# Block 1's mixer outputs are transposed through the bank of the projections' transposes

## The chip, the cores and the metric

The kernel runs on one core of a Trainium2 chip. The metric is the device time of one launch in microseconds (us), here on that one core. TensorE is called PE in the rows, VectorE DVE, ScalarE ACT, GpSimd POOL and SyncE SP; PEld is TensorE's weight load.

## The reference

The reference is a small transformer with two kinds of blocks over 1024 tokens of width 1024. Only the first kind ("block 1", two layers) matters here. In each of its layers a normed input goes through one wide projection, its columns feed three mixers, and the mixers' outputs stand side by side and go through the output projection:

```python
ATTN_W = 512; RET_W = 256; GLA_W = 256          # D_MIX = 1024
o = attention: softmax over a window of 128 keys, 8 heads of 64   # rotary on q and k, gate g
o = retention: 4 heads of 64, chunks of 128, fixed decay          # head norm, gate
o = gated_linear_attention: 4 heads (dk 32, dv 64), learned decay # head norm, gate
y = concat([attn, ret, gla]) @ w_out                              # then a norm and the residual
```

Every product is made of fp32 operands that are split into a high and a low part (three matmuls for one), so each operand that meets a weight exists as a pair: `hi` is a rounded copy and `lo` is what the copy lost.

## The kernel before, in words

A layer's 1024 tokens are worked in two halves of four token tiles of 128. So block 1 has four halves, in the order (layer 0, first), (layer 0, second), (layer 1, first), (layer 1, second). The block takes about the first 1300 us of the launch; what follows it has its own code and does not call the changed function.

For each half the host code writes out, in this order: `p_attn` (three projections: K and V, then Q, then the gate G), the output product of the half before (`finish`), `p_ret` (retention's projections), `p_gla` (the projections of gated linear attention, GLA, and between two of them `norm_T`, which norms and transposes the next half's input). The mixers themselves are generators: `s_attn`, `s_ret` and `s_gla` of a half are appended to a list, and after each k step of any projection `tick` runs one step of the generator that stands first. So GLA of one half is worked while the K, Q and G projections of the next half run. Priorities (`HP`, `HE`, `HX`) and a scheduler turn this into one fixed order of instructions for each engine.

When a token tile of a mixer is finished, `into` (L534) transposes it on PE into PSUM and `split` (L201) evacuates it twice: ACT casts it into the high part (L202), DVE subtracts that from PSUM for the low part (L203). It runs for 16 attention tiles (4 transposes each), 16 retention tiles and 16 GLA tiles (2 transposes each), 48 in all. The pair is called M, and the output product reads it.

PSUM has eight banks, and the tiles that share a tag take turns in its banks in the order in which the host code allocates them:

```python
mk("ps", {"mm": 4, "mt": 1, "sm": 2, "o": 1}, space=PSUM)     # L176
```

`mm` holds the four accumulators of a projection, one for each token tile. `sm` (two banks) holds the scores of the three mixers (L721, L726, L746, L846, L997), their state updates (L867, L1018) and, before the change, the 48 transposes of `into`. `mt` (one bank) holds the transposes of rotated queries and keys (L524 with source pe), the decays of GLA and the transposes of `norm_T` (L398). `o` holds the mixers' outputs.

Two more places matter below. When the Q projection ends, each token tile's query is rotated by DVE (`rotary`, twice per token tile, for two groups of heads: L650, L653 and L654 read the accumulator, L655 and L656 write the result) and then transposed through `mt`; the accumulator is free for the G projection after the second L654. The rotary uses the SBUF tag `pe`, which has three buffers: the result, and two of the products. And in `s_gla` the first two GLA tiles reach `into` while the host code is still in the Q projection of the next half, so they are allocated ahead of the queries' transposes.

Of the kernel before, what the change touches and what calls it, by code (L numbers as in the profile page):

```python
# [162 lines left out]
class Net:  # L163
# [369 lines left out]

    def into(self, mT, k0, t, src, n):  # L534
        hi, lo, _ = mT
        ps = self.transposes(None, src, n)
        ts_ = slice(t * P, (t + 1) * P)
        self.split(hi(k0, k0 + n)[:, :, ts_], lo(k0, k0 + n)[:, :, ts_], ps)

# [1190 lines left out]
```

## Time and profile before

| what | value |
|---|---|
| median of 3 runs | 3937.48 us (3937.02 to 3942.3) |
| the profiled execution | 3937.08 us, its span 3935.3 us |
| mean granted clock of PE | 0.986 of full speed |
| PE / DVE / ACT / POOL busy | 95% / 62% / 43% / 17% of the span |

The span runs from the first to the last instruction; the profiled execution's own time is 1.8 us longer and lies within the range of the three runs. The shares are averages over the launch.

### The profile page before, as it was taken

The numbers are of one execution on the slowest core, as the hardware profiler recorded it, in microseconds if no ns is written. First come the engines' busy times: TensorE is split into PE (matmuls) and PEld (weight loads), VectorE is DVE, ScalarE is ACT, GpSimd is POOL, SyncE is SP. The second block draws the span as 40 slices with busy tenths as digits, with TensorE's granted clock in tenths as the row PEclk, the third lists the DMA queues.
The fourth block names the chain that finished last, engine by engine and source line by source line (L and its number), as shares of the span: only waits on it lengthen the run. The fifth ranks groups of instructions, "written<-read, shape, count | busy, mean of one in ns | idle before, by whom it ended". The sixth has DMA issues, their size and how long they took to land. (4 is left out here: it accounts for less than half of the span.)

```text
span 3935.3 us, 55613 instructions
## 1 busy us (share of the span) xinstructions
PE 3726.1 (95%) x19144; PEld 3045.4 (77%) x19144; DVE 2445.6 (62%) x5209; ACT 1685.8 (43%) x3652; POOL 649.3 (17%) x1026
## 2 busy tenths in 40 slices
PE   7999999999999898899999999999899999999998
PEld 6877777877877787677887788888777788887886
DVE  7686787687687657576545643335765654455444
ACT  4443444454454555464334422224554543344333
POOL 2021134243252212131001000000311100001000
PEclk9999999999999999999999999999999999999999
DMA  6144344343343313333333632222412123334332
GB/s 213 50 134 121 113 143 121 109 129 110 105 136 98 103 56 107 108 108 105 126 102 110 209 110 68 62 66 89 145 54 86 69 64 97 97 100 166 97 97 94
DMA packets 249453, 420.37 MB, mean 107 GB/s; under 512 B 32002, under 2 KB 101203, under 8 KB 249171
## 3 DMA queue, kind: packets, MB, share of 16 engines
q1 hardware_dynamic: 241426, 389.52, 32.0%
q0 software_dynamic: 7744, 27.30, 1.9%
q8 instruction: 151, 2.47, 0.3%
q14 instruction: 132, 1.07, 0.1%
HBM read 389.42 MB, written 27.30 MB: 106 GB/s over the span
## 5 line engine op out<-in xcount | busy, mean ns | idle before, releaser
L203 DVE TENSOR_TENSOR wl<-wr,wh 128x512 fp32r<-128x512 f32 (+2 forms) x948 | 644.2, 682 | 812.9 <-ACT wh L202 809.4
L202 ACT CAST wh<-wr 128x512 fp32r<-128x512 f32 (+2 forms) x948 | 553.7, 585 | 1208.8 <-PE mm L502 489.8
L502 PE MATMUL mm<-wh,M 128*128 128x512 f32 (+1 forms) x2944 | 945.9, 393 | 24.6 <-ACT M L202 14.8
L502 PE MATMUL mm<-wh,H 128*128 128x512 f32 (+2 forms) x2432 | 791.5, 396 | 12.3 <-DVE pe L654 3.6
L506 PE MATMUL mm<-H,wh 128*128 128x512 f32 x2240 | 727.4, 395 | 1.8 <-ACT wh L202 1.7
L502 PEld LDWEIGHTS mm<-wh,M 128*128 128x128 f32 x2944 | 550.0, 190 | 142.8 <-ACT M L202 23.1
L502 PE MATMUL mm<-wl,M 128*128 128x512 f32 (+1 forms) x1472 | 576.0, 391 | 0.4 <-DVE wl L203 0.4
L502 PEld LDWEIGHTS mm<-wh,H 128*128 128x128 f32 x2432 | 450.0, 192 | 100.5 <-issue 4.7
L506 PEld LDWEIGHTS mm<-H,wh 128*128 128x128 f32 x2240 | 418.8, 189 | 82.2 <-ACT wh L202 2.0
L502 PE MATMUL mm<-wl,H 128*128 128x512 f32 (+2 forms) x1216 | 471.1, 388 | 0.0
L506 PE MATMUL mm<-H,wl 128*128 128x512 f32 x1120 | 444.5, 397 | 0.0
L502 PEld LDWEIGHTS mm<-wl,M 128*128 128x128 f32 x1472 | 279.8, 190 | 49.2 <-DVE wl L203 1.2
L502 PEld LDWEIGHTS mm<-wl,H 128*128 128x128 f32 x1216 | 234.0, 192 | 35.1 <-issue 0.2
L506 PEld LDWEIGHTS mm<-H,wl 128*128 128x128 f32 x1120 | 212.2, 189 | 37.2
L1398 PEld LDWEIGHTS o<-kv,pT 128*128 128x128 f32 x1280 | 158.1, 192 | 25.0 <-ACT pT L1394 20.4
L317 POOL TENSOR_TENSOR ac<-ac,aw 128x256 f32<-128x256 f32 x168 | 142.9, 851 | 162.8 <-ACT aw L316 143.9
L1398 PE MATMUL o<-kv,pT 128*128 128x64 f32 x1280 | 167.5, 274 | 1.6 <-ACT pT L1394 0.9
L311 DVE SCALAR_TENSOR_TENSOR ac<-aw,c,ac 128x256 f32<-128x256 f32 x280 | 160.1, 572 | 5.9 <-DMA aw<-in_w_ada 3.1
L1483 DVE TENSOR_TENSOR Z<-Z,mm 128x512 f32<-128x512 f32 x224 | 140.2, 681 | 2.8 <-PE mm L502 2.5
L558 POOL TENSOR_TENSOR tm<-tm 128x1 f32<-128x1 f32 x34 | 6.6, 196 | 763.3 <-ACT pe L553 762.9
L1375 DVE CUSTOM_DVE_ANT_0 p<-sm,c,c 128x384 f32<-128x384 f32 (+1 forms) x144 | 82.2, 571 | 76.0 <-PE sm L1373 74.5
L1381 ACT ACTIVATE p<-p,ti 128x640 f32<-128x640 f32 (+2 forms) x144 | 110.8, 770 | 43.1 <-DVE ti L1380 39.7
(353 smaller groups left out, 5703.1 us busy)
## 6 DMA issues: line engine op xcount, KB each, us to landing
wr<-in_w_ff SPq DMA_DIRECT2D x512, 256.0 KB, 2.7
wr<-in_w_in SPq DMA_DIRECT2D x240, 256.0 KB, 2.7
wr<-in_w_out SPq DMA_DIRECT2D x144, 256.0 KB, 2.7
x<-xd SPq DMA_DIRECT2D x64, 512.0 KB, 4.9
aw<-in_w_ada SPq DMA_DIRECT2D x192, 128.0 KB, 2.1
x<-in_w_ada SPq DMA_DIRECT2D x96, 256.0 KB, 2.9
xd<-x POOLq DMA_DIRECT2D x44, 512.0 KB, 3.8
wr<-in_w_in SPq DMA_DIRECT2D x152, 128.0 KB, 2.1
```

Of the source, the lines that this page charges most:

```text
L202: self.nc.scalar.copy(hi, src)
L203: self.nc.vector.tensor_sub(lo, src, hi.bitcast(F32))
L311: nc.vector.scalar_tensor_tensor(acc[:, 0], wt, c[0], acc[:, 0], ALU.mult, ALU.add)
L317: nc.gpsimd.tensor_tensor(acc[:, 1], acc[:, 1], wt, ALU.add)
L502: nc.tensor.matmul(acc[j][:, :ncol], lhsT=x[:, j * P:(j + 1) * P], rhs=y[:, :ncol], start=first, stop=last)
L506: nc.tensor.matmul(acc[j][:m, :w], lhsT=y[:, j * P:j * P + m], rhs=x[:, :w], start=first, stop=last)
L558: nc.gpsimd.tensor_tensor(ss[j][:, 0:1], ss[j][:, 0:1], ss[j][:, 1:2], ALU.add)
L1375: nc.vector.tensor_tensor_reduce(sc[:, at:at + w], ps[:, :w], mask, 1.0, prev, ALU.add, ALU.max, accum_out=acc)
L1381: nc.scalar.activation(sc[:, :at], sc[:, :at], AF.Exp, bias=nm, accum_out=den[:, h:h + 1])
L1398: nc.tensor.matmul(O[:, h * 64:h * 64 + 64], lhsT=pT[:, i, :], rhs=Vs(j)[:, sl], start=i == 0, stop=i == nk - 1)
L1483: nc.vector.tensor_add(y, y, ps)
```

## The change

`into` allocates its PSUM tile from the tag `mt` where it allocated it from `sm`. Nothing else is edited; the number of instructions and their shapes stay the same.

```diff
     def into(self, mT, k0, t, src, n):
         hi, lo, _ = mT
-        ps = self.transposes(None, src, n)
+        ps = self.transposes(None, src, n, tag="mt")
         ts_ = slice(t * P, (t + 1) * P)
         self.split(hi(k0, k0 + n)[:, :, ts_], lo(k0, k0 + n)[:, :, ts_], ps)
```

What moves is the order. DVE at the handover from the Q to the G projection of the second half, before (mm_2941 is the Q accumulator of token tile 1, pe_3316 its rotated query, sc_3163 a GLA output):

```order
L650 TENSOR_TENSOR pe_3317<-mm_2941,c_158 128x256
L653 TENSOR_TENSOR pe_3318<-mm_2941,c_160 128x4x32
L654 TENSOR_TENSOR pe_3318<-mm_2941,c_160 128x4x32
L655 TENSOR_TENSOR pe_3316<-pe_3317,pe_3318 128x4x32
L656 TENSOR_TENSOR pe_3316<-pe_3317,pe_3318 128x4x32
L827 TENSOR_TENSOR sc_3163<-sc_3163,ti_3169 128x256
L650 TENSOR_TENSOR pe_3324<-mm_2941,c_158 128x256
L653 TENSOR_TENSOR pe_3325<-mm_2941,c_160 128x4x32
L654 TENSOR_TENSOR pe_3325<-mm_2941,c_160 128x4x32
```

The same place on DVE now: the first L654 of that tile, the first two of the rows behind it, and the last ones up to its second L654:

```order
L654 TENSOR_TENSOR pe_3318<-mm_2941,c_160 128x4x32
L1021 SCALAR_TENSOR_TENSOR gs_2546<-gs_2547,ti_2550,sm_3157 32x64 x4
L820 TENSOR_TENSOR sc_3163<-o_3151,pu_2504 128x256
...
L203 TENSOR_TENSOR M_1108<-mt_3267,M_1107 128x2x128
L311 SCALAR_TENSOR_TENSOR ac_3230<-aw_3243,c_70,ac_3230 128x256
L1000 COPY_PREDICATED st_2966<-c_629,sm_3290 128x512
L655 TENSOR_TENSOR pe_3316<-pe_3317,pe_3318 128x4x32
L656 TENSOR_TENSOR pe_3316<-pe_3317,pe_3318 128x4x32
L311 SCALAR_TENSOR_TENSOR ac_3230<-aw_3246,c_70,ac_3230 128x256
L650 TENSOR_TENSOR pe_3324<-mm_2941,c_158 128x256
L653 TENSOR_TENSOR pe_3325<-mm_2941,c_160 128x4x32
L654 TENSOR_TENSOR pe_3325<-mm_2941,c_160 128x4x32
```

Between the two L654 stood 5 rows, and now stand 24: GLA's scores and updates, a head norm (L820, L824, L827), two low parts of M and seven rows of the modulation (five of them L311).

PE at the same place, before (mm_3382 and mm_3383 are the first two accumulators of the G projection):

```order
L502 MATMUL mm_3382<-wh_3518,H_2262 128x512
L502 MATMUL mm_3382<-wl_3519,H_2262 128x512
L502 MATMUL mm_3382<-wh_3518,H_2263 128x512
L502 MATMUL mm_3383<-wh_3386,H_2256 128x512
L502 MATMUL mm_3383<-wl_3387,H_2256 128x512
L524 MATMUL mt_3332<-c_76,pe_3316 128x128 x4
```

PE at the same place now (mt_3267 is the tile of the second GLA `into`, mt_3310 and mt_3332 those of the queries of token tiles 0 and 1):

```order
L502 MATMUL mm_3382<-wh_3518,H_2263 128x512
L283 MATMUL o_3226<-c_76,ac_3084 128x1 x2
L524 MATMUL mt_3267<-c_76,sc_3163 128x128 x2
L997 MATMUL sm_3255<-sc_3206,sc_3204 128x256 x2
L1011 MATMUL o_3404<-gs_2546,gq_2552 128x256
L997 MATMUL sm_3290<-sc_3265,sc_3263 128x256 x2
L524 MATMUL mt_3310<-c_76,pe_3294 128x128 x4
L1018 MATMUL sm_3410<-pu_2509,gq_2580 128x256
L1014 MATMUL o_3404<-pu_2509,st_2966 128x64 x4
L1018 MATMUL sm_3479<-pu_2515,gq_2580 128x256
L502 MATMUL mm_3383<-wh_3386,H_2256 128x512
```

Between the two accumulators 9 rows of GLA, of `into` and of a query's transposes have moved in. The handovers of the third and fourth halves have the same shape, with 46 and 25 DVE rows from one L654 to the other where 6 rows stood.

The third place is the beginning of `norm_T` for the second half, on PE. Before (o_1776 is an attention output, mm_1900 and mm_1901 are accumulators of GLA's first projection):

```order
L755 MATMUL o_1776<-kv_267,sc_1853 128x64
L757 MATMUL o_1776<-kv_267,sc_1855 128x64
L398 MATMUL mt_2272<-c_76,x_2220 128x128
L506 MATMUL mm_1901<-H_142,wl_1915 128x512
L506 MATMUL mm_1901<-H_143,wh_1914 128x512
L506 MATMUL mm_1900<-H_144,wh_1946 128x512
L398 MATMUL mt_2272<-c_76,x_2229 128x128
```

And now (mt_2148 is the tile of retention's third `into`, mm_2344 an accumulator of GLA's second projection):

```order
L524 MATMUL mt_2148<-c_76,sc_2115 128x128 x2
L867 MATMUL sm_2160<-pu_1892,pu_1504 128x128 x2
L502 MATMUL mm_2344<-wh_2407,H_146 128x512
L502 MATMUL mm_2344<-wl_2408,H_146 128x512
L860 MATMUL o_2153<-rs_1934,sc_2134 128x128 x2
L862 MATMUL o_2153<-pu_1892,st_2125 128x64 x3
L398 MATMUL mt_2272<-c_76,x_2220 128x128
L398 MATMUL mt_2272<-c_76,x_2229 128x128
```

`norm_T` now starts behind retention's third `into` and in the next projection. Between its first and its last transposes stood 91 matmuls of projections (38 L506 and 53 L502), and now stand 36. In the passes of the first, third and fourth halves it moves alike (to 36, 47 and 47 matmuls); in that of the second half 11 L506 and 42 L502 in two groups become 44.

## Rows read from the trace of the kernel before

**Rows 1.** The page, busy time of each engine and its share of the span.

```profile
PE 3726.1 (95%) x19144; PEld 3045.4 (77%) x19144; DVE 2445.6 (62%) x5209; ACT 1685.8 (43%) x3652; POOL 649.3 (17%) x1026
```

**Rows 2.** Windows, block 1: stretch, PE, PEld, DVE, ACT, POOL busy, clock, DMA, GB/s.

```profile
50.00:1250.00 1200.00, 1129.31 (x6073) 914.58 (x6072) 929.18 (x2084) 558.84 (x1362) 350.55 (x497) 0.99 0.38 116
```

**Rows 3.** Groups of PE instructions, 50 to 1290 us: busy, mean ns, idle before.

```profile
L997 PE MATMUL sm<-sc,sc 128*128 128x256 f32 x224 | 64.7, 408 | 22.4 <-DVE sc L989 19.6 <-DVE gs L1021 2.1 <-DVE md L286 0.5
L398 PE MATMUL mt<-c,x 128*128 128x128 f32 x158 | 28.8, 288 | 4.8 <-DVE x L377 3.6 <-DVE pe L403 0.9 <-ACT pe L401 0.2
L524 PE MATMUL sm<-c,sc 128*128 128x128 f32 x144 | 25.9, 278 | 13.9 <-DVE sc L827 12.4 <-DVE st L1000 1.1
```

**Rows 4.** Timeline of PE, G's second accumulator: start, duration, idle before and releaser.

```profile
316.44 0.47 PE L502 MATMUL mm<-wh,H 128*128 128x512 f32 x1 [0.32 <-DVE pe L654]
...
606.88 0.48 PE L502 MATMUL mm<-wh,H 128*128 128x512 f32 x1
```

**Rows 5.** Timeline of DVE at the handovers of the second and third halves.

```profile
314.21 0.29 DVE L654 TENSOR_TENSOR pe<-mm,c 128x128 f32<-128x128 f32 x1
...
316.01 0.28 DVE L654 TENSOR_TENSOR pe<-mm,c 128x128 f32<-128x128 f32 x1
...
603.20 0.28 DVE L654 TENSOR_TENSOR pe<-mm,c 128x128 f32<-128x128 f32 x1
...
604.36 0.47 DVE L311 SCALAR_TENSOR_TENSOR ac<-aw,c,ac 128x256 f32<-128x256 f32 x1
604.76 0.41 DVE L650 TENSOR_TENSOR pe<-mm,c 128x256 f32<-128x256 f32 x1
...
605.29 0.28 DVE L654 TENSOR_TENSOR pe<-mm,c 128x128 f32<-128x128 f32 x1
```

**Rows 6.** Timeline of DVE, one step of GLA's chain in the third half.

```profile
625.89 0.41 DVE L824 TENSOR_REDUCE ti<-sc 128x4 f32<-128x256 f32 x1
626.22 0.41 DVE L203 TENSOR_TENSOR M<-sm,M 128x256 fp32r<-128x256 f32 x1
628.00 0.62 DVE L827 TENSOR_TENSOR sc<-sc,ti 128x256 f32<-128x256 f32 x1 [1.36 <-POOL ti L209]
628.53 0.70 DVE L1000 COPY_PREDICATED st<-c,sm 128x512 f32<-128x512 uint8 x1
629.13 0.41 DVE L987 TENSOR_TENSOR sc<-pt,sc 128x256 f32<-128x256 f32 x1
629.47 0.68 DVE L989 TENSOR_TENSOR sc<-st,sc 128x512 f32<-128x512 f32 x1
630.07 0.21 DVE L286 TENSOR_TENSOR md<-o,c 128x2 f32<-128x2 f32 x2
```

**Rows 7.** Windows from each handover to the end of GLA.

```profile
316.40:349.00 32.60, 30.17 (x154) 24.29 (x155) 28.67 (x78) 11.27 (x22) 2.56 (x4) 1.00 0.43 130
602.10:655.00 52.90, 47.24 (x233) 37.03 (x234) 47.09 (x112) 25.35 (x53) 26.08 (x38) 1.00 0.36 108
907.90:975.00 67.10, 62.69 (x294) 49.16 (x295) 52.22 (x114) 32.78 (x68) 24.20 (x33) 1.00 0.39 120
```

**Rows 8.** Timeline of PE, the last GLA `into` of a half.

```profile
343.91 0.44 PE L524 MATMUL sm<-c,sc 128*128 128x128 f32 x2 [1.44 <-DVE sc L827]
```

**Rows 9.** Groups, M's evacuation: DVE by shape in 60 to 1250 us, ACT in all.

```profile
L203 DVE TENSOR_TENSOR M<-sm,M 128x256 fp32r<-128x256 f32 x32 | 13.4, 418 | 3.0 <-ACT M L202 2.7
L203 DVE TENSOR_TENSOR M<-sm,M 128x512 fp32r<-128x512 f32 x16 | 11.0, 688 | 0.4 <-ACT M L202 0.3
L202 ACT CAST M<-sm 128x256 fp32r<-128x256 f32 (+1 forms) x48 | 20.9, 436 | 42.6 <-PE sm L524 42.4
```

**Rows 10.** Timeline of PE, a retention `into` in the first half.

```profile
237.43 0.44 PE L524 MATMUL sm<-c,sc 128*128 128x128 f32 x2 [1.63 <-DVE sc L827]
```

**Rows 11.** Windows of 2 us behind that wait.

```profile
238.00:240.00 2.00, 2.00 (x14) 2.00 (x13) 1.63 (x3) 0.28 (x1) 1.03 (x2) 0.61 0.16 34
240.00:242.00 2.00, 2.00 (x10) 1.60 (x8) 1.68 (x6) 0.04 (x1) 0.00 (x0) 0.54 0.14 35
```

## The prediction

> **What bounds the kernel now.** I read the page's busy times first: PE is busy 95% of the span, DVE 62% [rows 1], so over the launch PE sets the time. The change touches block 1 alone, so the windows come next: between 50 and 1250 us PE is busy 1129 of 1200 us, DVE 929 [rows 2]. There is some 71 us of PE idle time, and what ends it is a chain on DVE: GLA's scores wait for L989 (19.6 us), the transposes of finished mixer tiles for L827 of the head norm (12.4 us) [rows 3]. So I price the change as PE idle time in block 1 added or taken away, and look where the order of PE and DVE moves. I count 0.2%, 7.9 us, as what a measurement of this kernel can tell from no change.
>
> **What the change does, part by part.** No instruction is added or removed. The 48 tiles leave two banks, which the scores share, for one bank, which the queries' transposes and `norm_T` share, and the tiles of one bank are worked strictly in the order of the host code. ACT's casts and DVE's subtractions are the same ones. The DMAs are the same too; on SP's and POOL's queues a few weight and modulation loads change places by some rows, which I price at nothing, because the weights are prepared ahead; if that cover were gone, a late load would show as PE waiting for L202.
>
> *The handover from Q to G (halves two, three and four).* Query transposes now come behind the second GLA `into` in the one bank. That `into` waits for a head norm; behind it on PE wait the query's transposes, GLA's updates, and then G's second accumulator. On DVE the rotary's L655 waits, since the three `pe` buffers are full until a query has been transposed; behind it wait L650, L653 and the second L654, which is what frees that accumulator. Before, the two L654 started 1.80 us apart (314.21 and 316.01) and 2.09 us apart (603.20 and 605.29) [rows 5]; the fourth half has the first pattern again, for which I take 1.7. Now the distance is the DVE work that has moved in between. I price it start to start: L311 0.40 (604.36 to 604.76, [rows 5]); L1000 0.60, L989 0.60, L987 0.34, L824 0.33 and L827 0.53, each to the next start [rows 6]; L203 of M and L820 0.34, like L824; the short L1021 0.2, L286 0.1 and L309 0.3 as estimates from their nearest rows, L286's 0.21 for two and L824.
>
> - Half two: 5 L311, 3 L1000, 2 L989, 2 L987, L824, L827, 2 M, L820, 4 L1021, L286, L309: 2.0+1.8+1.2+0.7+0.3+0.5+0.7+0.3+0.8+0.1+0.3 = 8.7, with the rotary's own 1.3 (the 1.80 without an L827) 10.0 us.
> - Half three: 13 L311, 5 L1000, 4 L989, 4 L987, 2 L824, 2 L827, 2 M, L820, 4 L1021, 4 L286, 2 L309: 5.2+3.0+2.4+1.4+0.7+1.1+0.7+0.3+0.8+0.4+0.6 = 16.6, with the rotary 17.9 us.
> - Half four: like half two with one L1021 and two L286: 8.2, with the rotary 9.5 us.
>
> That is 8.2, 15.8 and 7.8 us more than before. DVE also waits inside such a stretch: L824 to L827 goes through POOL, 1.36 us of waiting [rows 6], and a score's matmul stands between L989 and L1000, about 1 us. So 2.4 us once in halves two and four, and 3.6 us in half three with its two head norms and one of the score waits hidden. The first rotary itself stands 1.2 and 0.6 us earlier in DVE's order in halves two and three and 3.0 later in half four. G's second accumulator started 0.32 us after a wait in half two, without slack, and 1.3 us after the L654 had ended in half three (605.57 to 606.88) [rows 4, 5]. So it starts later by 8.2+2.4-1.2 = 9.4, by 15.8+3.6-0.6-1.3 = 17.5 and by 7.8+2.4+3.0 = 13.2 us. In that time PE does work that it otherwise did later (the scores, updates and transposes that moved in, at 0.2 us each as a pair of transposes takes 0.44 [rows 8] and 0.35 for scores of 256 columns): 3.9, 8.5 and 4.8 us. Extra idle time is 5.5+9.0+8.4 = 22.9 us.
>
> *What comes back.* The GLA work done early cannot hold PE up later. From the handovers to the end of GLA PE was idle 2.4, 5.7 and 4.4 us [rows 7], 12.5 in all, so no more than that returns there. The wait of the last `into` for its head norm, 1.44 us [rows 8] and about 1.5 in each of the other halves, has the same chain ahead of it and stays. I take 12.5-4.5 = 8.0 back; the bounds are 0 and 12.5, or all of the 22.9 if later stretches, too, are bound by DVE.
>
> *norm_T in halves one, three and four.* It starts later, behind retention's third `into`, and 36 to 47 projection matmuls stand inside it where 91 stood, so each step's evacuation has less cover. Half two's pass had 42 already, and in all passes of block 1 together PE waited 1.1 us for the evacuations (0.9 L403, 0.2 L401) [rows 3]. So at most about 1.1 for each newly pressed pass, at least nothing: I take 1.5 for the three, since 36 is tighter than 42.
>
> *Retention's part* comes some us earlier and has the `sm` banks to itself; its `into` waited 1.63 us for L827 [rows 10] and two others waited like it, about 5 us together. I take half back, 2.5 us, with bounds 0 and 5.
>
> *The clock.* Behind that 1.63 us wait the granted clock read 0.61 and then 0.54 [rows 11], so PE ran near the lower of its two levels for some of 4 us: 0.4 of the speed lost is 1.7 us. Other waits of this length left it at 1.00. The three new idle stretches could each pay this (5.1) or none: I take 1.
>
> The sum is 22.9-8.0+1.5-2.5+1.0 = +14.9 us. On the profiled execution's own 3937.08 us, 0.4 under the median of the runs, that is **3952 us**.
>
> **A rule weighed against the rows.** In the rows, an evacuation of these tiles costs a cast of 0.44 and a subtraction of 0.42 to 0.69 us [rows 9], and PE went on with other tiles meanwhile. The Trainium skill's page "Perfetto Trace Analysis", section "Matmuls", says that independent groups should rotate through several PSUM banks, so that one group's evacuation lies beside the next one's matmuls; a single bank gives that up. The trace of before cannot show one bank for these tiles; the rival that follows from the rule is D.
>
> **The rivals.**
>
> - *A, the forecast:* slower, by 8 to 24 us, 3945 to 3961. Chance 0.50.
> - *B, the idle time only moves.* In the stretches behind the handovers DVE is busy 28.7 of 32.6 and 47.1 of 52.9 us [rows 7], nearly as much as PE. If DVE bounds both engines, work that it does early is given back in full, behind GLA too. For it: this occupancy. Against it: PE waits only 12.5 us there, less than the 22.9 added. It gives -2 to +8, some 3940. Chance 0.26.
> - *C, faster: two relieved banks.* A third of the groups in `sm` leaves it. If scores run further ahead of DVE, part of the 19.6+12.4 = 32 us of waits [rows 3] goes; a third of it is 11 us, 3926. It decides if the handovers cost less than that, which they do if the queries' transposes find the GLA tile finished by the time that they are due. Against it: these waits are for data from DVE and not for a bank. Chance 0.11.
> - *D, one bank exposes each evacuation.* If PE stood still at each of the 48 tiles for cast and subtraction, 20.9+13.4+11.0 = 45.3 us [rows 9], 3982. This is what the page's rule would make of the change; against it, PE's order has other matmuls between one `mt` tile and the next outside the handovers and `norm_T`. Chance 0.05.
> - *E, the clock falls at each handover and in norm_T,* 5 to 10 us on top of the forecast, 3957 to 3963. Chance 0.08.
>
> **How the numbers follow.** The predicted time is A's. Range 3936 to 3966: below it lie most of C and the better edge of B (about 0.13), above it D and the worst of E (0.07). Slower by over 0.2% means over 3945: D, E, nearly all of A and a little of B, 0.62. Faster by over 0.2% means under 3930: most of C, 0.10. The rest is 0.28.
>
> **What would show it.** In the changed kernel's trace, the two L654 of token tile 1 should start about 12, 21 and 12 us apart (waits included), and G's second accumulator should wait for L654 for several us, at about 320, 615 and 920 us; the stretch from there to the end of GLA should hold less idle time than before. Retention's wait at 237 us should be shorter, and L398's waits for L403 and L401 above 1.1 us. After block 1 nothing differs. I am wrong if the L654 stand apart as forecast but block 1 ends no later (B), if they do not (C), or if the transposes of `into` wait on L203 all over block 1 (D). The weakest term is what comes back.

## The result and the profile after

The change makes the kernel slower: 3972.51 us median (3968.33 to 3974.35, four runs) against 3937.56 us, a ratio of 1.0085 with a 95% interval of 1.0067 to 1.0102. The forecast was the right way, 3952, but less than half the size (+14.9 for +35): the time lies above the range.

The profiled execution took 3968.33 us, 31 more than that of before. The page's first line:

```profile
PE 3742.8 (94%) x19144; PEld 3057.4 (77%) x19144; DVE 2440.0 (62%) x5209; ACT 1688.2 (43%) x3652; POOL 652.2 (16%) x1026
```

With the same number of instructions PE is busy 16.7 us longer than in [rows 1], and DVE no longer. So only a part of the loss can be waiting. The windows from the end of the first half's attention projections to the same projection matmul behind block 1 say where to look; first the kernel before, then the changed one (stretch, PE, PEld, DVE, ACT, POOL busy, clock, DMA share, GB/s):

```profile
112.80:1324.60 1211.80, 1141.10 (x6141) 923.58 (x6142) 925.18 (x2053) 569.84 (x1391) 360.16 (x523) 0.99 0.38 115
```

```profile
112.40:1358.50 1246.10, 1156.80 (x6142) 934.23 (x6143) 921.23 (x2053) 572.42 (x1391) 362.59 (x523) 0.97 0.37 112
```

The stretch is 34.3 us longer, of which 15.7 is PE's busy time and 18.6 idle time (70.7 before, 89.3 now); outside it the two kernels differ by 3 us the other way. The clock fell from 0.99 to 0.97. The G projections of halves two, three and four, each from its first matmul to the first one of the output product behind it, before:

```profile
312.60:348.60 36.00, 33.29 (x170) 26.53 (x169) 32.03 (x91) 11.81 (x24) 5.04 (x8) 1.00 0.41 122
602.10:641.50 39.40, 35.32 (x172) 27.22 (x172) 36.55 (x90) 17.70 (x36) 16.65 (x24) 1.00 0.36 108
903.70:942.20 38.50, 35.10 (x171) 26.37 (x171) 36.11 (x94) 18.30 (x38) 13.73 (x20) 1.00 0.36 109
```

The same three stretches in the changed kernel:

```profile
312.70:355.20 42.50, 35.69 (x173) 27.77 (x173) 35.86 (x100) 12.77 (x26) 5.46 (x8) 0.96 0.41 117
605.00:664.40 59.40, 49.87 (x218) 38.06 (x218) 48.76 (x119) 24.85 (x52) 27.51 (x42) 0.83 0.32 98
926.30:973.40 47.10, 40.22 (x184) 31.06 (x184) 37.77 (x98) 19.40 (x42) 16.48 (x23) 0.89 0.32 100
```

The column to look at is the last but two: at all three handovers the granted clock was at full speed before, and is 0.96, 0.83 and 0.89 now. Between the same projection matmuls, 34.1 us of these three stretches lie at the lower level now, and none did before. The two L654 of the held token tile, which the prediction named, stand on DVE's timeline now so (start, duration):

```profile
314.39 0.28 DVE L654 TENSOR_TENSOR pe<-mm,c 128x128 f32<-128x128 f32 x1
...
328.34 0.28 DVE L654 TENSOR_TENSOR pe<-mm,c 128x128 f32<-128x128 f32 x1
...
606.47 0.27 DVE L654 TENSOR_TENSOR pe<-mm,c 128x128 f32<-128x128 f32 x1
...
632.81 0.27 DVE L654 TENSOR_TENSOR pe<-mm,c 128x128 f32<-128x128 f32 x1
...
928.18 0.28 DVE L654 TENSOR_TENSOR pe<-mm,c 128x128 f32<-128x128 f32 x1
...
941.42 0.27 DVE L654 TENSOR_TENSOR pe<-mm,c 128x128 f32<-128x128 f32 x1
```

They are 14.0, 26.3 and 13.2 us apart, where 1.8 and 2.1 us stood [rows 5]; forecast were about 12, 21 and 12. What PE does in the first of these stretches (duration, then the idle time before it):

```profile
316.64 0.60 PE L283 MATMUL o<-c,ac 128*128 128x1 f32 x4 [0.95 <-ACT sc L822]
319.60 0.44 PE L524 MATMUL mt<-c,sc 128*128 128x128 f32 x2 [2.35 <-DVE sc L827]
...
324.72 1.13 PE L997 MATMUL sm<-sc,sc 128*128 128x256 f32 x4 [1.38 <-DVE sc L989]
...
328.68 0.50 PE L502 MATMUL mm<-wh,H 128*128 128x512 f32 x1
```

PE's longest wait is that of the second GLA tile for its head norm (L827), in the middle of the queue, and G's second accumulator starts at 328.68, 12.2 us later than in [rows 4] and without a wait of its own. In the third half the clock was low for most of the handover, as windows of 5 us show:

```profile
605.00:610.00 5.00, 3.56 (x17) 2.74 (x18) 3.94 (x10) 1.02 (x2) 3.34 (x6) 1.00 0.36 107
610.00:615.00 5.00, 5.00 (x20) 4.30 (x21) 4.06 (x10) 2.58 (x6) 2.36 (x4) 0.53 0.27 78
615.00:620.00 5.00, 3.43 (x8) 1.74 (x6) 4.27 (x11) 2.04 (x5) 3.03 (x4) 0.50 0.26 81
620.00:625.00 5.00, 2.90 (x11) 2.44 (x12) 3.86 (x11) 2.19 (x6) 3.65 (x8) 0.50 0.27 82
625.00:630.00 5.00, 3.59 (x11) 2.39 (x11) 3.90 (x8) 1.53 (x3) 1.66 (x3) 0.76 0.16 52
```

PE was idle for 1.4 us in the first of them and ran at 0.50, its lower level, for the next three. What that does to one group of matmuls, on PE's timeline shortly before the fall and inside it:

```profile
599.00 1.03 PE L997 MATMUL sm<-sc,sc 128*128 128x256 f32 x4
...
617.40 2.04 PE L997 MATMUL sm<-sc,sc 128*128 128x256 f32 x4 [1.02 <-DVE sc L989]
```

A group of four score matmuls of one shape takes twice as long. That gives an account which I use for every kernel below. Over the stretch above (the 289th to the 3601st projection matmul, so that each kernel is cut at the same work) I sum PE's busy time that lay in stretches at the lower level, by the trace's record of the granted clock, and call half of it lost; what is left of the busy time is the work at full clock. The column "low clock" is all the time at the lower level in the stretch, idle or busy:

| kernel | ratio to before (95%) | idle, us | low clock, us | lost by it, us | work at full clock, us |
|---|---|---|---|---|---|
| before | 1 | 70.7 | 24.7 | 11.9 | 1129.3 |
| the change | 1.0085 (1.0067 to 1.0102) | 89.3 | 68.9 | 30.8 | 1126.0 |
| gla_only | 1.0066 (1.0052 to 1.0080) | 85.5 | 72.6 | 31.5 | 1124.3 |
| gla01_sm | 1.0033 (1.0022 to 1.0043) | 82.3 | 48.4 | 23.3 | 1125.1 |
| ret_only | 1.0031 (1.0018 to 1.0043) | 80.8 | 37.5 | 17.4 | 1128.2 |
| attn_only | 1.0008 (0.9998 to 1.0018) | 79.2 | 31.1 | 15.2 | 1123.0 |
| ys_after | 1.0024 (1.0014 to 1.0034) | 80.4 | 38.1 | 18.6 | 1126.8 |
| ys_before | 1.0020 (1.0009 to 1.0030) | 72.6 | 34.8 | 17.1 | 1126.0 |
| fill | 1.0098 (1.0080 to 1.0115) | 84.8 | 48.2 | 23.3 | 1139.5 |
| late4 | 1.0013 (1.0003 to 1.0023) | 78.3 | 35.1 | 16.8 | 1125.9 |
| late16 | 1.0088 (1.0073 to 1.0104) | 95.9 | 69.3 | 25.8 | 1123.7 |
| late_nofill | 1.0059 (1.0045 to 1.0072) | 82.1 | 72.4 | 31.1 | 1129.0 |
| late_fill | 1.0047 (1.0034 to 1.0059) | 70.4 | 31.5 | 15.4 | 1148.9 |

Ratios are over the timed runs beside those of the kernel before on the same chip; the other columns are of the one profiled execution of each kernel. So small differences in them say little: the work at full clock, which should not differ between the kernels without added matmuls, spreads from 1123.0 to 1129.3, and the mean granted clock of the kernel before runs from 0.982 to 0.988 over its timed runs. The change's is 0.979 or 0.980 in all four. The expectations count low clock over a slightly longer stretch, 72 us for the change and 27 before. The change added 18.6 us of idle time and 18.9 us lost to the clock, and 3.3 us less is left as work at full clock: 34.2 in all.

### The profile page after: what moved, and what is told of

The parts are those of the page before. It is cut to its first block, busy times and chain, and to the rows that moved or that the text cites. A ratio compares the mean times of both kernels' runs of the same rounds, so it can differ in the third digit from the quotient of the medians.

```text
span 3966.6 us, 55560 instructions
## 1 busy us (share of the span) xinstructions
PE 3742.8 (94%) x19144; PEld 3057.4 (77%) x19144; DVE 2440.0 (62%) x5209; ACT 1688.2 (43%) x3652; POOL 652.2 (16%) x1026
## 5 line engine op out<-in xcount | busy, mean ns | idle before, releaser
L203 DVE TENSOR_TENSOR wl<-wr,wh 128x512 fp32r<-128x512 f32 (+2 forms) x948 | 636.6, 673 | 823.8 <-ACT wh L202 819.8
L502 PE MATMUL mm<-wh,M 128*128 128x512 f32 (+1 forms) x2944 | 944.4, 393 | 22.8 <-ACT M L202 14.8
L502 PE MATMUL mm<-wh,H 128*128 128x512 f32 (+2 forms) x2432 | 792.1, 397 | 9.9 <-DVE pe L654 3.0
L506 PE MATMUL mm<-H,wh 128*128 128x512 f32 x2240 | 726.4, 395 | 1.5 <-ACT wh L202 1.4
L502 PEld LDWEIGHTS mm<-wh,M 128*128 128x128 f32 x2944 | 549.5, 190 | 139.4 <-ACT M L202 23.0
L502 PE MATMUL mm<-wl,M 128*128 128x512 f32 (+1 forms) x1472 | 575.3, 391 | 0.4 <-DVE wl L203 0.4
L502 PEld LDWEIGHTS mm<-wh,H 128*128 128x128 f32 x2432 | 451.6, 193 | 97.8 <-DVE pe L1241 3.4
L506 PEld LDWEIGHTS mm<-H,wh 128*128 128x128 f32 x2240 | 418.9, 189 | 81.3 <-ACT wh L202 1.7
L502 PE MATMUL mm<-wl,H 128*128 128x512 f32 (+2 forms) x1216 | 475.0, 391 | 1.4 <-DVE wl L203 1.4
L506 PE MATMUL mm<-H,wl 128*128 128x512 f32 x1120 | 443.6, 396 | 0.0
L502 PEld LDWEIGHTS mm<-wl,M 128*128 128x128 f32 x1472 | 280.0, 190 | 50.0 <-DVE wl L203 1.1
L502 PEld LDWEIGHTS mm<-wl,H 128*128 128x128 f32 x1216 | 235.3, 193 | 37.1 <-DVE wl L203 1.8
L506 PEld LDWEIGHTS mm<-H,wl 128*128 128x128 f32 x1120 | 211.6, 189 | 38.0
L311 DVE SCALAR_TENSOR_TENSOR ac<-aw,c,ac 128x256 f32<-128x256 f32 x280 | 155.3, 555 | 6.9 <-DMA aw<-in_w_ada 3.4
L1375 DVE CUSTOM_DVE_ANT_0 p<-sm,c,c 128x384 f32<-128x384 f32 (+1 forms) x144 | 82.1, 570 | 76.9 <-PE sm L1373 75.6
L1381 ACT ACTIVATE p<-p,ti 128x640 f32<-128x640 f32 (+2 forms) x144 | 110.9, 770 | 40.9 <-DVE ti L1380 37.5
```

What stands on the lines that cost most here:

```text
L203: self.nc.vector.tensor_sub(lo, src, hi.bitcast(F32))
L311: nc.vector.scalar_tensor_tensor(acc[:, 0], wt, c[0], acc[:, 0], ALU.mult, ALU.add)
L502: nc.tensor.matmul(acc[j][:, :ncol], lhsT=x[:, j * P:(j + 1) * P], rhs=y[:, :ncol], start=first, stop=last)
L506: nc.tensor.matmul(acc[j][:m, :w], lhsT=y[:, j * P:j * P + m], rhs=x[:, :w], start=first, stop=last)
L1375: nc.vector.tensor_tensor_reduce(sc[:, at:at + w], ps[:, :w], mask, 1.0, prev, ALU.add, ALU.max, accum_out=acc)
L1381: nc.scalar.activation(sc[:, :at], sc[:, :at], AF.Exp, bias=nm, accum_out=den[:, h:h + 1])
```

## Experiments

Two theories stood first. H: the loss is made at the handovers, where queries' transposes queue behind two GLA tiles in one bank, the rotary's three buffers fill, and the accumulator comes late. S: one bank exposes every tile's evacuation, so that the loss spreads over all 48 tiles. The first four runs put part of the tiles back.

**gla_only**: only GLA's tiles in mt.

```diff
-        ps = self.transposes(None, src, n, tag="mt")
+        ps = self.transposes(None, src, n, tag="mt" if k0 == 6 else "sm")
```

> Only the 16 GLA tiles go through the one bank mt; attention's and retention's stay in sm. The order has 18, 45 and 30 DVE rows between the two L654 of the held token tile, as in the change (24, 46, 25), and norm_T stands as before (91 matmuls inside it). Theory H (the loss is made at the handovers, where the queries' transposes queue behind two GLA tiles): about +25 us on the kernel before, 3957 to 3968, with the granted clock low for some 60 us of block 1 against 27 before. Rival S (each tile in a single bank exposes its evacuation, so that the loss spreads over the 48 tiles): a third of the loss, +10 to +13, about 3949.

Measured 3962.67 against 3935.55 us, +27: H. A third of the tiles makes three quarters of the loss, with the whole of the clock's (31.5 us, where the change has 30.8).

**gla01_sm**: all but the first two GLA tiles of each half in mt.

```diff
+        ps = self.transposes(None, src, n, tag="sm" if k0 == 6 and t < 2 else "mt")
```

> The change, but the first two GLA tiles of each half stay in sm: 40 of 48 tiles go through mt. The order has 5 or 6 DVE rows between the two L654 everywhere, and norm_T is pressed as in the change (36 to 47 matmuls inside it). Theory H: +2 to +7 us on the kernel before, 3939 to 3945, low clock about as before. Rival S: five sixths of the loss, about +29, 3966. Rival N (the pressed norm_T and retention's tiles cost most): +15 or more, over 3952.

Measured 3948.61 against 3935.55 us, +13. Two tiles of a half put back take away most of the loss, which speaks for H, but what stays is more than H allowed and nearer to N: retention and `norm_T` cost something of their own.

**attn_only**: only attention's tiles in mt.

```diff
+        ps = self.transposes(None, src, n, tag="mt" if k0 == 0 else "sm")
```

> Only the 16 attention tiles go through mt. No DVE row moves between the two L654, and norm_T has 74 to 85 matmuls inside where 91 stood. Theory H: no change, 3934 to 3942. Rival S: a third of the loss or, as these tiles are twice as large, up to half: +12 to +17, 3949 to 3954.

Measured 3939.5 against 3935.55 us; the interval holds 1. Sixteen of the 48 tiles, and the largest, go through the one bank at no cost that the timed runs can tell from nothing, though PE was idle 8.5 us longer in the profiled execution. S falls.

**ret_only**: only retention's tiles in mt.

```diff
+        ps = self.transposes(None, src, n, tag="mt" if k0 == 4 else "sm")
```

> Only the 16 retention tiles go through mt; the handovers stand as before, and norm_T is pressed exactly as in the change (36, 44, 47, 47 matmuls inside). If retention's tiles, allocated ahead of norm_T, are what presses it, and if that is what is left beside the handovers: +6 to +13 us on the kernel before, 3942 to 3949, most of it as PE idle time from retention's third tile to the end of norm_T, some 2 us in each half. Rival: pressing norm_T costs nothing and the rest comes of attention's tiles: no change, 3933 to 3939.

Measured 3945.51 against 3932.18 us, +13, at the upper edge of the forecast: this is what was left of gla01_sm, whose `norm_T` stands in the same order. PE's group for `norm_T`'s transposes in this run, 50 to 1330 us (busy, mean ns, idle before):

```profile
L398 PE MATMUL mt<-c,x 128*128 128x128 f32 x188 | 31.5, 286 | 11.1 <-DVE pe L403 6.7 <-DVE x L377 3.6 <-ACT pe L401 0.8
```

The waits for the evacuations (L403 and L401) are 7.5 us where 1.1 stood [rows 3], but 3.2 of them lie in a fifth pass behind the fourth half, at 1245 to 1328 us; gla01_sm shows these too, and the change has 0.3 there. The rest of the 13 is idle time spread over the projections and 5.5 us of clock. In GLA's two projections, where `norm_T` stands, idle time rose by 3.4 of 10.1 us, so the cost is as forecast, but most of it lies elsewhere. The single costs of GLA (27), retention (13) and attention (4) add up to 44, more than the change's 35; they may overlap, but the intervals do not show it.

**ys_after**: the change, with the rotated query in a buffer of another tag, so that the rotary can go on while queries wait for the bank.

```diff
         def evac_q(t, ps):
             tb = g * GT + t
-            q = self.T("pe", [P, 512])
+            q = self.T("ys", [P, 512])
```

> The change with all 48 tiles in mt, but the rotated query is written to a buffer of the tag ys, which lies idle until the output product, in place of pe. The queries' transposes still queue behind the GLA tiles, yet DVE no longer needs them to go on: 4 rows stand between the two L654 at every handover. Theory H in its full form (the loss runs through the three pe buffers: rotary waits, so the accumulator comes late, so G starts late): +2 to +7 us on the kernel before, 3939 to 3945, or less if the stalls that the kernel before had there (2.6 and 0.3 us) go as well. Rival Q (the bank itself holds PE up: whatever DVE does, PE waits in order at the GLA tile): +20 to +30, 3958 to 3968.

Measured 3944.32 against 3935.55 us, +9, a little above H's bounds and far below Q's. All 48 tiles still share the bank; only the buffer that tied the rotary to it is gone, and with it three quarters of the loss. So most of the way from bank to time goes through the `pe` buffers, as the prediction had it. In what is left, the longest wait of PE at the third half's handover is one for GLA's scores, on its timeline, with the clock around it:

```profile
637.63 1.22 PE L997 MATMUL sm<-sc,sc 128*128 128x256 f32 x2 [4.32 <-DVE sc L989]
```

```profile
630.00:635.00 5.00, 3.31 (x15) 2.28 (x14) 4.93 (x10) 3.17 (x6) 1.48 (x3) 1.00 0.31 99
635.00:640.00 5.00, 2.37 (x7) 1.90 (x8) 3.96 (x8) 2.19 (x6) 2.78 (x4) 0.69 0.46 140
640.00:645.00 5.00, 5.00 (x27) 4.36 (x26) 3.10 (x8) 2.61 (x5) 1.22 (x3) 0.62 0.26 76
```

**ys_before**: the same edit on the kernel before.

> The kernel before with the rotated query in ys in place of pe: all tiles in sm. It takes away the rotary's wait for a buffer (PE waited 2.6 us for L655 and L656's readers and 3.6 us for L654 in four places). Theory H: faster by 0 to 6 us, 3930 to 3936; it shows whether the change with ys (3944) lost its time to mt or gained some from ys. Rival: the waits move to GLA's chain, no change.

Measured 3939.36 against 3932.18 us: slower by 0.2%, where I had forecast 0 to 6 us faster. PE's waits for L654 fell only from 3.6 to 2.9 us, since the longest, at the third half's first accumulator, stayed (2.21 us where 2.55 stood); PE's idle time did not fall (72.6 against 70.7), and 5.2 us more were lost to the clock in this execution. Neither the theory's gain nor a version worth keeping. It also says that ys_after gained nothing from the new buffer as such: with the query in ys, the kernel stands at 1.0020 without the shared bank and at 1.0024 with it.

The next question was the clock: does PE's standing still draw it down (C), or something else (R)?

**fill**: the change, with identity matmuls ahead of the transposes of the first two GLA tiles.

```diff
+        ps = self.T("mt", [P, n, P])
+        for j in range(8 if k0 == 6 and t < 2 else 0):
+            self.nc.tensor.matmul(ps[:, j % 2, :], lhsT=self.k1("ident"), rhs=self.k1("ident"), start=True, stop=True)
+        for j in range(n):
+            self.nc.tensor.transpose(ps[:, j, :], src[:, j * P:(j + 1) * P], self.k1("ident"))
```

> The change, and 8 matmuls of the identity with itself go into the bank of each of the first two GLA tiles of a half, ahead of its transposes, which overwrite them. They lie where PE waited for the head norm (2.35 us in the second half). The result is the reference's. The handover keeps its shape (19, 38 and 20 DVE rows between the two L654 where the change has 24, 46 and 25). Theory C (PE standing still at the handover is what lets the granted clock fall, and the low clock is half of the loss): block 1 has under 45 us of low clock where the change has 72, and the time falls under the change's in spite of more matmuls, to 3950 to 3965. Rival R (the clock falls for another reason, for instance the mix of small matmuls): 65 to 75 us of low clock, and the fillers cost up to 1.6 us each for eight tiles: 3972 to 3985.

Measured 3970.61 us, a ratio like the change's. Low clock fell from 68.9 to 48.2 us, between the two forecasts, and gave back 7.5 us; idle time fell by 4.5; but the fillers added 13.5 us of work, since a part of them lay where PE had not stood still. Not decided: the order had moved too.

**late16**: the kernel before, every tile in sm, with the accumulator held up by copies on DVE, which hold up GLA's chain there too.

```diff
             for e in range(2):
+                for _ in range(16 if t == 1 and e == 1 and (l, g) != (0, 0) else 0):
+                    nc.vector.tensor_copy(qv[:, 1], ps.rearrange("p (u pr hf d) -> p u pr hf d", u=2, pr=4, hf=2)[:, 1])
                 self.rotary(lambda i: qv[:, e, :, i, :], ps[:, e * 256:(e + 1) * 256], 4, tb, 0)
```

> The kernel before, with all tiles in sm, but DVE copies a part of the Q accumulator 16 times into the tile of the rotated query (128x256 each, overwritten by the rotary) between the two rotary groups of token tile 1 in halves two to four: the second L654 comes 5 to 6 us later by the copies alone, 35 DVE rows stand between the two. Theory H with C (the late accumulator and nothing else makes the loss, and PE's idle time draws the clock down): PE idle time up by 6 to 15 us in block 1, low clock up by 20 to 45 us, the time up by 12 to 30, 3948 to 3966. Rival M (the loss needs the shared bank: transposes waiting in it): the GLA work covers the copies and the time stays within +5, 3936 to 3941. Rival R (idle time costs itself alone): idle and time rise alike, low clock as before.

Measured 3965.85 against 3932.18 us, +34, the change's own loss without the shared bank, and more than the 12 to 30 that were forecast. Theory H with C; the added time is 25.2 us of idle time, above the forecast, and 13.9 lost to the clock. M falls, and so does R of this run, with 69.3 us of low clock. The waits have another shape than the change's: PE's longest at the handovers are 6.9 us for L654 and 6.2 for GLA's scores.

**late4**: four copies in place of sixteen.

> As the run with 16 copies, with 4: the second L654 comes 1.4 us later by the copies, 11 DVE rows between the two. If each us by which the accumulator is late costs alike, a quarter of the loss of 16 copies, +6 to +10 us. If the loss begins only where PE stands still for longer, as the kernel before showed with its 2.55 us wait at 602 us behind which the clock read 1.00: 0 to +4 us, low clock as before.

Measured 3939.23 against 3934.64 us, +5, 0.13% with an interval that begins at 0.03%: between the two forecasts. It does not decide whether the loss is proportional.

**late_nofill** and **late_fill**: as late16, with four small copies more, each of which is read by 1 matmul or by 8 whose result nobody reads. DVE's order is the same in both, and PE's differs by these matmuls, by the rows of GLA beside which some of them stand, and by two projection matmuls of the third half that change places with L283.

```diff
+                late = t == 1 and e == 1 and (l, g) != (0, 0)
+                if late:
+                    mark, fp = self.T("ys", [P, 512]), self.T("mt", [P, 4, P])
...
+                    if i % 4 == 0:
+                        nc.vector.tensor_copy(mark[:, i * 32:i * 32 + P], ps[:, 256:256 + P])
+                        for j in range(8):      # 1 in late_nofill
+                            nc.tensor.matmul(fp[:, j % 4, :], lhsT=self.k1("ident"), rhs=mark[:, i * 32:i * 32 + P], start=True, stop=True)
```

> A control for the next run. The kernel before with the second L654 of token tile 1 held up on DVE, as in the run with 16 copies: 16 copies of 128x256 and 4 of 128x128 between the two rotary groups, and 4 matmuls of 128 columns on PE that read the 4 small copies and whose result nobody reads. As with the 16 copies alone: 25 to 35 us over the kernel before, some 20 to 27 us more PE idle time in block 1, 30 to 45 us more low clock.

> The same as the control, but each of the 4 small copies is read by 8 matmuls in place of 1: 28 more matmuls of 128 columns at each of the three handovers, in the same places of PE's order, behind the same waits, and DVE's order is the same. They only take up time in which PE stood still for DVE. Theory C (PE's standing still lets the clock fall): low clock at least 20 us shorter than the control's, and the time 4 to 12 us under the control's although there is more work. Rival R (the clock falls for another reason): low clock as in the control, within 7 us, and the time the same or up to 10 us longer.

Measured 3958.18 us (3954.66 to 3962.57) without and 3953.78 us (3947.76 to 3955.26) with the 84 more matmuls, both beside 3934.64. The control missed its forecast: +23.5 us for 25 to 35, with 11.4 us more idle time for 20 to 27 and 47.7 more low clock for 30 to 45. It has the low clock that the test needs. The windows of the handovers, without the fillers:

```profile
918.50:960.00 41.50, 34.13 (x150) 26.95 (x151) 36.61 (x104) 14.42 (x30) 12.81 (x19) 0.84 0.28 83
306.40:353.00 46.60, 39.08 (x181) 30.77 (x181) 40.35 (x115) 12.40 (x24) 4.86 (x8) 0.89 0.35 105
607.00:660.00 53.00, 46.61 (x201) 37.57 (x202) 45.84 (x119) 20.37 (x41) 19.74 (x30) 0.81 0.30 90
```

And with them:

```profile
919.40:960.00 40.60, 37.57 (x216) 31.15 (x217) 38.60 (x107) 16.03 (x33) 14.07 (x21) 1.00 0.29 88
311.50:356.00 44.50, 41.12 (x236) 33.87 (x235) 39.21 (x113) 11.84 (x23) 4.86 (x8) 1.00 0.35 106
610.00:660.00 50.00, 46.73 (x256) 38.00 (x256) 44.29 (x119) 20.39 (x42) 19.42 (x31) 0.97 0.31 95
```

Each answer begins with half four. The clock stays up: in halves two, three and four it reads 1.00, 0.97 and 1.00 in place of 0.89, 0.81 and 0.84. PE does 20 us more work in block 1, its idle time falls by 11.7 and what the clock takes by 15.7 us; the median is 4.4 us lower with more work, at the lower edge of what C forecast. The clock is the firmer of the two signs: its mean over a run is 0.980 to 0.983 in the six runs without and 0.984 to 0.987 in the six with the fillers, while one run without them is faster than two with them. R falls. One place of the fourth half on PE's timeline, without the fillers:

```profile
925.02 0.49 PE L695 MATMUL mt<-ys,c 128*128 128x128 f32 x2
927.66 0.80 PE L695 MATMUL mt<-ys,c 128*128 128x128 f32 x2 [2.15 <-DVE ys L693]
929.84 2.08 PE L1006 MATMUL sm<-sc,sc 128*128 128x256 f32 x4 [1.38 <-DVE gs L1030]
```

And the same place with them:

```profile
925.95 2.05 PE L695 MATMUL mt<-ys,c 128*128 128x128 f32 x16
928.59 2.05 PE L695 MATMUL mt<-ys,c 128*128 128x128 f32 x16 [0.59 <-DVE ys L693]
930.77 1.13 PE L1006 MATMUL sm<-sc,sc 128*128 128x256 f32 x4
931.74 1.95 PE L695 MATMUL mt<-ys,c 128*128 128x128 f32 x16
```

The scores (L1006, which is L997 of the kernel before) waited 1.38 us and took 2.08 us in the control; behind the fillers they wait for nothing and take 1.13 us.

The Trainium skill's page "TensorE: Matmul & The Clock Gate", section "A second HAM failure mode: psum-queue depth-cycling", describes a kernel whose PE micro-idles between groups of matmuls, often enough that the clock falls and rises again and again. These traces agree: in the handover of half three in the change no single wait of PE was longer than 1.8 us, and the clock read 0.50 to 0.53 for three windows of 5 us.

## Why the prediction was wrong

- **The mechanism at the handover was right, one sign of it was not.** The two L654 moved apart as named (14.0, 26.3, 13.2 for 12, 21, 12); GLA's tiles alone carry three quarters of the loss, and taking the `pe` buffer out of the chain takes most of it away. The handover of half three was undersized by 5 us, and in it the small matmuls of the chain ran at half speed. But G's second accumulator was to wait for L654 for several us, and in no half does PE wait in front of it. PE waits in the rows of GLA that now stand ahead of it. Its waits in the G projection of half three (us in all, times, longest), before, where none is for L827, and now:

```profile
PE mm L502 <- DVE pe L654: 2.5, 1, 2.5
...
PE sm L997 <- DVE sc L989: 0.7, 1, 0.7
```

```profile
PE mt L524 <- DVE sc L827: 2.5, 2, 1.4
PE sm L997 <- DVE sc L989: 2.4, 2, 1.4
PE mm L502 <- DVE pe L654: 2.0, 2, 1.8
```

- **The step that failed is the clock.** The prediction took one lapse behind a single 1.63 us wait [rows 10, 11] and allowed 1 us, with 5.1 at most. The account shows 18.9 us: low clock rose from 24.7 to 68.9 us. Of the 18.9, 14.2 were lost in the three G projections, where the kernel before lost nothing. The price of a lone wait says nothing of a stretch of some 15 to 25 us in which PE stands still again and again. That the bank is not needed for it is shown by late16 (all in sm, the same loss), and that PE's standing still does it by the pair with and without fillers. Rival E had this mechanism, at 5 to 10 us and a chance of 0.08: right cause, half its size.
- **The idle time at the handovers** was put at 22.9 us, of which 8.0 were to come back. In the G projections it rose by 12.9 us (4.07, 5.43 and 3.44 between the same projection matmuls), and 4.0 came back in the output products behind; net 8.9 where the prediction had 14.9. Both terms were too large. With the 14.2 us of clock the three stretches lost 27.1, so a part of the waiting that was forecast may have taken the form of slow work; no run separates the two. This error hid a part of the clock's: with the idle time as forecast the miss would have been larger.
- **norm_T and retention** were to give 1.0 us (1.5 less 2.5). They cost: 5.8 us of idle time in GLA's two projections in the change, and 13 us as a whole when retention's tiles alone go through the bank. The waits of `norm_T` for L403 and L401 rose from 1.1 [rows 3] to 4.6 us in the change, as PE's groups in 50 to 1330 us show:

```profile
L398 PE MATMUL mt<-c,x 128*128 128x128 f32 x159 | 26.0, 280 | 8.3 <-DVE pe L403 4.4 <-DVE x L377 3.7 <-ACT pe L401 0.2
L524 PE MATMUL mt<-c,sc 128*128 128x128 f32 x128 | 24.2, 288 | 19.6 <-DVE sc L827 18.3 <-POOL sc L770 0.6 <-DVE M L203 0.5
```

- **Retention's waits did not vanish.** The tiles' transposes wait 18.3 us for L827 in the second row, where 12.4 stood [rows 3]. Taken one by one on PE's timeline, retention's waits are 6.3 us before and 6.8 now, and GLA's 6.1 and 11.5. The scores' waits for L989 did not fall either (19.6 before, 21.7 now): freeing `sm` for them gave nothing back. That is rival C's ground, and it fell with it.
- **Rival D** fell: PE waited 0.5 us for L203 of M in all 128 transposes of that row, and 1.7 us in attn_only, which cost nothing that can be measured. The bank's evacuation was not the price; the order that a shared bank forces was. So the rule of the Trainium skill's page "Perfetto Trace Analysis", section "Matmuls", to rotate groups through several banks for the sake of the evacuation, does not bear on these tiles.
- **Rival B** fell: of the 12.9 us of idle time, 4.0 were given back.

What stays open: how the loss grows with the lateness (late4 lies between), where most of retention's 13 us comes from and why ys_after, which has retention's tiles in the one bank too, is hardly slower than ys_before, and why ys_before is slower by 0.2%.

## What to carry to other kernels

Tiles that share one bank are worked in the order in which the code allocates them, so before two producers are put on one bank, look at where their orders cross and what the later one holds up: here a query waiting for a GLA tile held an accumulator through a buffer of the rotary, while the 16 attention tiles went through the same bank at no cost that the runs can tell from nothing. Price a stretch in which PE waits again and again twice, as idle time and as work at the lower clock: over block 1 the second was as large here as the first (18.9 and 18.6 us). And when the order of two engines has to be kept for a test, change only how much work stands behind a wait that is already there, as the pair with fillers did.

## What the runs showed of the hardware that was not expected

Work that nobody needs made a kernel faster than its control, though not than the kernel before: 84 more matmuls of 128 columns, in places where PE waited for DVE, brought the low clock of block 1 from 72.4 to 31.5 us and the median from 3958.18 to 3953.78 us. And waits of 1 to 2 us each were enough: in the handover of half three the clock read 0.53, 0.50 and 0.50 over three windows of 5 us, while the longest single wait of PE was 1.79 us.
